# S5 input weights from two turned factors that are read back from DRAM with replication, in a hybrid encoder layer on Trainium2

## The chip, the cores and the metric

The kernel runs on one core of one Trainium2 chip. The metric is the device time of one execution in microseconds (us); the median of the runs is compared. The engines are TensorE (PE, whose weight loads are the row PEld), VectorE (DVE), ScalarE (ACT), GpSimd (POOL) and SyncE (SP). SP and POOL issue the DMAs.

## The reference, cut to what matters

One encoder layer over 512 tokens of 1024 channels: an input projection, two mixers in parallel (a bidirectional S5 state-space branch and a gMLP branch), a gated merge, cross-attention to 256 memory tokens, a SwiGLU FFN and a final norm, all in float32. The change is in the S5 branch. Its 512 channels are 32 groups (G) of 16 channels (C); each group has 64 complex states for each of two directions, so the 128 partitions hold direction and state.

```python
def s5_scan(u, lam_re, lam_im, log_step, b_re, b_im, c_re, c_im, reverse):
    lam = lax.complex(lam_re, lam_im)
    step = jnp.exp(log_step)[:, None]
    lam_bar = jnp.exp(lam * step)
    b_bar = ((lam_bar - 1.0) / lam)[..., None] * lax.complex(b_re, b_im)
    bu = jnp.einsum('gpc,lbgc->lbgp', b_bar, u)
    _, states = lax.associative_scan(_linear_recurrence, (a, bu), axis=0, reverse=reverse)
    return jnp.einsum('gcp,lbgp->lbgc', lax.complex(c_re, c_im), states).real
...
y = jax.nn.gelu(y); y = y * jax.nn.sigmoid(y @ w_glu)
merged = gate_a * (ya @ w_proj_a) + gate_b * (yb @ w_proj_b)
```

## The kernel before, in words

**The dense products.** Each float32 product is three products of split operands: ACT casts a weight block to fp32r (`whi`, L85), DVE makes the rest (`wlo`, L86), and PE takes hi x hi, hi x lo and lo x hi. Weight blocks of 512 KB stand in one `plan`. `next_w` hands out the next block; on the way it begins loads three blocks ahead (`LOADS`) and splits two blocks ahead (`SPLITS`). Three raw buffers rotate, so a load on SP's queue waits until the split of three blocks before has read its buffer.

**The weight sums.** w_proj_b, w_q and w_down use seven products in place of eight and need sums of weight blocks. `plan_sums` gives each of its 40 jobs a place in the plan and a step: at the place SP copies one block from DRAM to DRAM (L288), and `step` places later POOL adds another one by an accumulating DMA (L289). The first sixteen jobs are for w_proj_b and w_q. The plan's places run: 0 to 3 half of the v projection, 4 to 7 `u`, 8 to 11 the other half of v, 12 to 19 gate a, 20 to 27 the gMLP's u, 28 to 35 gate b, 36 to 49 w_proj_b, 50 and 51 w_glu.

**The S5 work beside them.** `s5_program` is a generator. `tick(us)` is called after each block with the PE time of that block; it grants credits at a rate of 0.8, and each `yield` of the generator spends some. A `yield None` gives up the rest of a tick. `later(n, f)` runs `f` after n units of 5.2 us of such product time. Thus the order in which instructions are written is fixed; a scheduler then places each engine's instructions by readiness in its own timeline, with that order as the priority. `in_order` pins an instruction, and `behind(ins, first)` orders one instruction after another on the same queue without a semaphore.

**The S5 inputs.** The scan is over 64 chunks of 8 steps (`Q`). For each chunk the state input is a product of u (128 rows: channel and step in the chunk) with weights W[(c, l), (direction, state)] for each group, real and imaginary. The weights are b_bar[state, c] times lam_bar's power [state, l]. Groups are taken in four octaves of eight (`NO`, `GO`). Before, `s5_inputs` makes for each octave and each of the two parts the weights with the state on the partitions: two broadcast products and a sum on DVE over 128 x 1024 (`inner` spreads b over l, `outer` the powers over c; L972, L974, L976), in the tile `wsx`. Then `turn` transposes the eight 128 x 128 blocks on PE (L951) and ACT copies them out of PSUM into `wt` (L952); `apply` multiplies with u (L958, tile `pz`); `keep` puts the result into `zh`, half by ACT (L963) and half by DVE (L964). An octave waits until the octave before has been turned.

**What follows.** When all eight halves are in `zh`, `s5_scan` runs 62 steps of four small DVE operations (L985 to L988). `s5_outputs` makes the outputs of each octave (`py` L1014, transposes `pyt` L1029, `y` L1034). `store_outputs` takes the gelu (L1046) and stores y to DRAM by POOL (`yd`, L1049). It is called three times between w_proj_b's products and once after `finish_side`, which runs out what is left. Then the tile `ygt` is loaded from `yd` by POOL (L1343), split (`yg_hi` L1349, `yg_lo` L1350), and w_glu's products read it.

`s5_kernels` makes the weights inside a chunk: `e` tiles (tags e0 and e1, two buffers each), the products `pk`, and for octaves 2 and 3 copies of e to DRAM (`ed`, L875) that are read back later. Slot A of SBUF holds `xt` at first, then `squares` (layer norm), then `sv`; slot E holds `wsx`.

Of the kernel before, what the change touches and what calls it, by code (L numbers as in the profile page):

```python
# [9 lines left out]
F32 = mybir.dt.float32  # L10
F32R = mybir.dt.float32r
AF = mybir.ActivationFunctionType
ALU = mybir.AluOpType
# [4 lines left out]
P = 128  # L18
D = 1024
T = 512  # L20
NT = T // P
# [18 lines left out]
Q = 8  # L40
# [12 lines left out]
def hybrid_layer_kernel(  # L53
# [26 lines left out]
    def aux(name, shape=(P, 512)):  # L80
        return pa.tile(list(shape), F32, tag="aux", name=name)
# [30 lines left out]
        cast[0] = split(hi, lo, src)  # L112
        return hi, lo

    cast = [None]

    def behind(ins, first):

# [20 lines left out]
    def plan_block(w, kb, k, c0, n, place=None, ordered=False, then=None, parts=1):  # L139
        got = {}  # L140

        def load():
            got["raw"] = wp.tile([P, k, n], F32, tag="raw", name="wraw", bufs=3)
            for i in range(0, k, k // parts):
                ins = nc.sync.dma_start(got["raw"][:, i:i + k // parts], block(w, kb + i, k // parts, c0, n))
                if ordered:
                    in_order(ins)

        def make():
# [182 lines left out]
    for i in range(4):  # L332
# [5 lines left out]
    plan_down(w_down, lambda q, c: down_tokens[0](q, c), down_plan)  # L338
    plan_units(UNITS, down_plan)

    plan_sums([(5, 3), (7, 3), (9, 2), (13, 5), (14, 5), (16, 4)] + [(18 + 2 * i, 3) for i in range(8)] +
              [(51 + 2 * i, 2) for i in range(4)] + [(85 + 3 * i, 3) for i in range(3)] +
              [(95 + 2 * i, 2) for i in range(3)] + [(122 + 4 * i, 4) for i in range(16)])
    used_w = [0]
# [112 lines left out]
    def later(n, fn):  # L457

        side["later"].append((side["now"] + n, fn))
# [228 lines left out]
    def s5_setup():  # L688
# [88 lines left out]
        st["pe"], st["pw"] = [], []  # L777
        for src in (pr, pi):
            pe = s5p.tile([P, G, Q], F32, name="pe%d" % len(st["pe"]))
            pw = s5p.tile([P, G, Q], F32, name="pw%d" % len(st["pw"]))  # L780
            A_.copy(pe[lo_], src[lo_, :, 0:Q])
            V.tensor_copy(pe[hi_], src[hi_, :, 0:Q][:, :, ::-1])
            V.tensor_copy(pw[lo_], src[lo_, :, 1:Q + 1])
            A_.copy(pw[hi_], src[hi_, :, 1:Q + 1][:, :, ::-1])
            st["pe"].append(pe)
            st["pw"].append(pw)
        ca = s5p.tile([P, 2, G], F32, name="ca")
        cb = s5p.tile([P, 2, G], F32, name="cb")
        for i in range(2):
# [35 lines left out]
        for t in st["bd"]:  # L825
            nc.gpsimd.memset(t, 0.0)
# [20 lines left out]
    def lc(t, g):  # L847
        return t[:, g].rearrange("p a b -> p (a b)")
# [84 lines left out]
            nc.sync.dma_start(glc(e), ed[o][i])  # L933
        load(o, es)

    turned = set()

    def s5_inputs(o):

        gs = slice(o * GO, (o + 1) * GO)  # L940
        br, bi = st["b"]
        pr, pi = st["pw"]
        zh, u = st["zh"], st["u"]

        def turn(i, e):
            turned.add((o, i))
            wt = s5p.tile([P, GO, P], F32, tag="wt", name="wt", bufs=2)
            for hf in range(2):
                ps = aux("pw", (P, 4, P))
                for j in range(4):  # L950
                    nc.tensor.transpose(ps[:, j, :], lc(e, 4 * hf + j), ident)  # L951
                nc.scalar.copy(wt[:, 4 * hf:4 * hf + 4, :], ps)  # L952
            later(0.5, lambda: apply(i, wt))

        def apply(i, wt):
            ps = aux("pz", (P, GO, NCH))
            for g in range(GO):
                nc.tensor.matmul(ps[:, g, :], wt[:, g, :], u[:, o * GO + g, :], start=True, stop=True)  # L958
            zv = zh[:, :, i, gs].rearrange("p n g -> p g n")
            later(0.5, lambda: keep(zv, ps))  # L960

        def keep(zv, ps):
            nc.scalar.copy(zv[lo_], ps[lo_])  # L963
            V.tensor_copy(zv[hi_], ps[hi_, :, ::-1])  # L964
            st["nz"] = st.get("nz", 0) + 1

        for i in range(2):
            while o > 0 and (o - 1, i) not in turned:
                yield None
            e = wsx[:, 2 + i].rearrange("p g (c l) -> p g c l", c=C)  # L970
            w = s5p.tile([P, GO, C, Q], F32, tag="etmp", name="etmp2")
            V.tensor_tensor(e, inner(br, gs, Q), outer((pr, pi)[i], gs, C), ALU.mult)  # L972
            yield 1.1
            V.tensor_tensor(w, inner(bi, gs, Q), outer((pi, pr)[i], gs, C), ALU.mult)  # L974
            yield 1.1
            V.tensor_tensor(e, e, w, (ALU.subtract, ALU.add)[i])  # L976
# [148 lines left out]
    tokm(w_in, OFF_V + 512, xn, KD, zv_evac(1))  # L1125


    squares = slot("A", (P, NT, GW), F32, "squares")

    def layer_norm(t):  # L1130

        nm, ss, ms, r = (np_.tile([P, 1 + (k == "ss")], F32, tag=k, name=k, bufs=2) for k in ("nm", "ss", "ms", "r"))
        nc.vector.tensor_tensor(nm, zsum[:, t, 0:1], zsum[:, t, 1:2], ALU.add)
        nc.vector.tensor_scalar(nm, nm, -1.0 / GW, None, ALU.mult)
        z = zt[:, t, :]
        for i in range(2):
            sum_sq(ss[:, i:i + 1], z[:, HALF[i]], squares[:, t, HALF[i]], nm)
# [861 lines left out]
```

## Time and profile before

| what | value |
|---|---|
| median of 3 runs | 866.23 us (866.2 to 868.49) |
| the profiled execution | 865.49 us, its span 863.7 us |
| granted TensorE clock | 0.998 |
| PE, DVE, ACT, POOL busy | 99%, 76%, 54%, 10% of the span |
| DMA | 169.56 MB in 115752 packets |
| HBM | 159.71 MB read, 48.73 MB written |

The times are those of whole executions; all views come from the one profiled execution, whose span runs from the first to the last instruction. Busy PE time is modelled: a product's tail overlaps with the next product, so the starts, not the durations, tell what one costs. In the lines of groups, the number after the bar is the group's busy time in us, then the mean of one in ns, then the idle time of the engine just before it and what ended most of that.

### The profile page before, as it was taken

To read this page: it belongs to the slowest core of one execution; us is meant where nothing else is said; L and a number is where in the kernel's file an instruction comes from. 1 tells how busy PE (TensorE), PEld (TensorE's weight loads), DVE (VectorE), ACT (ScalarE), POOL (GpSimd) and SP (SyncE) were. 2 spreads that over 40 slices of the span, in tenths; PEclk is the share of its full clock that TensorE was granted. 3 is DMA by queue.
4 is the path that set the end of the run, shared out by engine and by line. 5 is a ranking of instruction groups with operands and counts; after the bars stand their busy time and mean duration, and the time that the engine had idled before them with its cause. 6 is when DMAs were issued, how large, how long until landed. Compare 5 with 4: busy or idle time off the path is not lost.

```text
span 863.7 us, 14764 instructions
## 1 busy us (share of the span) xinstructions
PE 856.1 (99%) x5780; PEld 766.6 (89%) x5780; DVE 660.5 (76%) x1076; ACT 466.1 (54%) x698; POOL 89.3 (10%) x119
## 2 busy tenths in 40 slices
PE   9999999999999999999999999999999999999997
PEld 7888888888889988889899888999999999988886
DVE  7698896899846768668758755867877768899875
ACT  6734853244355543557547544645545554656674
POOL 0002302111021110110010001010211111000000
PEclk9999999999999999999999999999999999999999
DMA  9759565987574798735696555557999898366564
GB/s 270 196 174 308 113 174 153 254 195 191 146 220 150 244 309 248 244 102 199 213 276 162 147 146 147 146 159 185 213 233 240 215 229 220 92 191 209 196 186 156
DMA packets 115752, 169.56 MB, mean 196 GB/s; under 512 B 9297, under 2 KB 80481, under 8 KB 115554
## 3 DMA queue, kind: packets, MB, share of 16 engines
q1 hardware_dynamic: 95330, 139.54, 49.3%
q0 software_dynamic: 20064, 28.55, 20.4%
q8 instruction: 45, 0.74, 0.3%
q10 hardware_dynamic: 288, 0.52, 0.2%
q14 instruction: 25, 0.20, 0.1%
HBM read 159.71 MB, written 48.73 MB: 241 GB/s over the span
## 4 chain that ended last, share of the span: by engine, by line
PE 99%; DVE 1%; ACT 0%; issue 0%
PE pf L374 27%; PE pt L374 18%; PE px L1238 13%; PE dx L374 7%; PE pq L1238 6%; PE dq L374 3%; PE pv L1238 3%; PE bx L1238 3%; PE qx L1238 3%; PE dv L374 2%; PE pz L958 2%; PE qv L1238 1%; PE po L374 1%; PE psc L374 1%; PE py L1014 1%; PE qq L1238 1%
## 5 line engine op out<-in xcount | busy, mean ns | idle before, releaser
L85 ACT CAST whi<-wraw 128x1024 fp32r<-128x1024 f32 x141 | 145.2, 1031 | 160.2 <-PE pf L374 54.8
L86 DVE TENSOR_TENSOR wlo<-wraw,whi 128x1024 fp32r<-128x1024 f32 x141 | 168.3, 1195 | 64.8 <-ACT whi L85 64.2
L374 PE MATMUL pf<-xn,whi 128*128 128x512 f32 x448 | 140.1, 392 | 0.0
L374 PEld LDWEIGHTS pf<-xn,whi 128*128 128x128 f32 x448 | 83.5, 188 | 16.9
L374 PE MATMUL pf<-xn,wlo 128*128 128x512 f32 x224 | 87.5, 391 | 0.0
L1238 PE MATMUL px<-fn,whi 128*128 128x256 f32 x480 | 83.4, 277 | 0.0
L1238 PEld LDWEIGHTS px<-fn,whi 128*128 128x128 f32 x480 | 72.5, 188 | 0.2
L86 DVE TENSOR_TENSOR wlo<-b,whi 128x1024 fp32r<-128x1024 f32 x40 | 48.9, 1223 | 26.0 <-ACT whi L85 26.0
L85 ACT CAST whi<-b 128x1024 fp32r<-128x1024 f32 x40 | 42.2, 1054 | 48.3 <-PE px L1238 27.7
L1238 PE MATMUL px<-fn,wlo 128*128 128x256 f32 x240 | 66.4, 277 | 0.0
L1238 PE MATMUL pq<-s,whi 128*128 128x256 f32 x320 | 55.0, 276 | 0.0
L374 PE MATMUL dx<-whi,s 128*128 128x512 f32 x166 | 52.2, 391 | 0.4 <-DVE h L1922 0.4
L86 DVE TENSOR_TENSOR wlo<-t,whi 128x1024 fp32r<-128x1024 f32 x30 | 36.7, 1225 | 18.4 <-ACT whi L85 18.4
L85 ACT CAST whi<-t 128x1024 fp32r<-128x1024 f32 x30 | 31.6, 1054 | 34.6 <-PE pv L1238 11.4
L374 PEld LDWEIGHTS pf<-xn,wlo 128*128 128x128 f32 x224 | 42.1, 188 | 8.7
L1238 PEld LDWEIGHTS pq<-s,whi 128*128 128x128 f32 x320 | 48.2, 188 | 0.0
L1238 PEld LDWEIGHTS px<-fn,wlo 128*128 128x128 f32 x240 | 45.1, 188 | 0.0
L1238 PE MATMUL pq<-s,wlo 128*128 128x256 f32 x160 | 44.2, 276 | 0.0
L374 PE MATMUL pt<-whi,xn 128*128 128x512 f32 x128 | 43.1, 402 | 0.0
L374 PEld LDWEIGHTS dx<-whi,s 128*128 128x128 f32 x166 | 31.1, 188 | 7.4 <-ACT whi L85 0.8
L374 PE MATMUL dx<-wlo,s 128*128 128x512 f32 x83 | 32.2, 389 | 0.0
L289 POOL DMA_DIRECT2D dsum<-in_w_down_dram x12 | 13.2, 1103 | 172.5 <-DMA dsum<-in_w_down_dram 167.4
(458 smaller groups left out, 2222.7 us busy)
## 6 DMA issues: line engine op xcount, KB each, us to landing
wraw<-in_w_in_dram SPq DMA_DIRECT2D x34, 512.0 KB, 4.6
dsum<-in_w_down_dram SPq DMA_DIRECT2D x20, 512.0 KB, 5.8
wraw<-dsum SPq DMA_DIRECT2D x20, 512.0 KB, 4.4
b<-in_w_gate_dram SPq DMA_DIRECT2D x15, 512.0 KB, 5.1
b<-in_w_up_dram SPq DMA_DIRECT2D x15, 512.0 KB, 4.7
wraw<-in_w_down_dram SPq DMA_DIRECT2D x15, 512.0 KB, 3.8
dsum<-in_w_down_dram POOLq DMA_DIRECT2D x10, 512.0 KB, 7.5
dsum<-dsum POOLq DMA_DIRECT2D x10, 512.0 KB, 7.9
```

Of the source, the lines that this page charges most:

```text
L85: hi = nc.scalar.copy(dst_hi, src)
L86: lo = nc.vector.tensor_tensor(dst_lo, src, dst_hi.bitcast(F32), ALU.subtract)
L289: plan[j + step][1].append((0, lambda d=dst, x=more: nc.gpsimd.dma_start(d, x, accum_op=ALU.add)))
L374: m = nc.tensor.matmul(ps, a[x], b[y], start=start and i == 0, stop=stop and i == 2, skip_group_check=free)
L958: nc.tensor.matmul(ps[:, g, :], wt[:, g, :], u[:, o * GO + g, :], start=True, stop=True)
L1014: in_order(nc.tensor.matmul(ps[64 * j:64 * j + 64, :, :, h, :].rearrange("p q d c -> p d q c"), a, b, start=k == ks[0], stop=k == ks[2], t ...
L1238: nc.tensor.matmul(ps[:, j, :], a[x], b[y], start=start and j == k == i == 0, stop=k == 3 and i == 2, skip_group_check=True)
```

## The change

The weights W are a product of two factors that depend on (c, state) and on (l, state). After the change each factor is turned once and written to DRAM with the state in the free direction; for each octave it is loaded back with replication, so that both lie in the layout (c, l) x (group, state), and DVE's two products and the sum give the weights already turned.

- In `s5_setup` the powers `pw` are laid out by octave, step and group, turned by four transposes and stored (`ptd`). `by_octave` copies b's real and imaginary part into that order, turns each by four transposes, and stores it (`btd`). The set-up yields 1.9 credits more.
- `load_factors(o)` issues four loads of 512 KB on SP for an octave: b with each row repeated over the eight steps, the powers with their eight rows repeated over the 16 channels. Even octaves go into slot A (`scr`) and `wsx`, odd ones into the e buffers. Octave 0 is loaded after the set-up, octave 1 one unit after u is there, octaves 2 and 3 three units after the inputs of 0 and 1 are written. The later ones are ordered behind the weight load that was issued last.
- `s5_inputs` has no `turn` any more: `apply` reads the sum itself.
- `plan_sums`: twelve of the first fourteen places move to later ones.
- Slot A is `scr` from the start of the S5 work on; the layer norm's squares of all four token tiles go to its first part.

```diff
-    plan_sums([(5, 3), (7, 3), (9, 2), (13, 5), (14, 5), (16, 4)] + [(18 + 2 * i, 3) for i in range(8)] +
+    plan_sums([(5, 3), (7, 3)] + [(15 + 2 * i, 3) for i in range(10)] + [(40, 3), (44, 3)] +
               [(51 + 2 * i, 2) for i in range(4)] + [(85 + 3 * i, 3) for i in range(3)] +
...
-            pw = s5p.tile([P, G, Q], F32, name="pw%d" % len(st["pw"]))
+            pw = s5p.tile([P, NO, Q, GO], F32, name="pw%d" % len(st["pw"]))
             A_.copy(pe[lo_], src[lo_, :, 0:Q])
             V.tensor_copy(pe[hi_], src[hi_, :, 0:Q][:, :, ::-1])
-            V.tensor_copy(pw[lo_], src[lo_, :, 1:Q + 1])
-            A_.copy(pw[hi_], src[hi_, :, 1:Q + 1][:, :, ::-1])
+            rows = pw.rearrange("p o q g -> p o g q")
+            by_octave = src[:, :, 1:Q + 1].rearrange("p (o g) q -> p o g q", o=NO)
+            V.tensor_copy(rows[lo_], by_octave[lo_])
+            A_.copy(rows[hi_], by_octave[hi_, :, :, ::-1])
...
+        yield 0.1
+        ps = aux("pbt", (P, 2, 2, P))
+        for i in range(2):
+            for k in range(2):
+                nc.tensor.transpose(ps[:, i, k, :], st["pw"][i].rearrange("p o q g -> p (o q g)")[:, P * k:P * k + P], ident)
+        rows = scr[:, 3, 0:512].rearrange("p (i k d) -> p i k d", i=2, k=2)
+        A_.copy(rows, ps)
+        for i in range(2):
+            nc.sync.dma_start(ptd[i].rearrange("(k q) d -> q k d", k=2), rows[:, i])
...
+        def by_octave(i, z):
+            t = scr[:, 1 + i, 0:512].rearrange("p (o c g) -> p o c g", o=NO, c=C)
+            A_.copy(t.rearrange("p o c g -> p o g c"), z.rearrange("p (o g) c -> p o g c", o=NO))
+            ps = aux("pbt", (P, NO, P))
+            for o in range(NO):
+                nc.tensor.transpose(ps[:, o, :], t[:, o].rearrange("p c g -> p (c g)"), ident)
+            rows = scr[:, 1 + i, 512:1024].rearrange("p (o d) -> p o d", o=NO)
+            A_.copy(rows, ps)
+            nc.sync.dma_start(btd[i].rearrange("o q d -> q o d"), rows)
...
         yield 1.8
+        by_octave(0, zr)
...
+        yield 1.8
+        by_octave(1, zi)
...
+    btd = [dp.tile([NO, P, P], F32, name=f"btd{i}") for i in range(2)]
+    ptd = [dp.tile([NO * Q * GO, P], F32, name=f"ptd{i}") for i in range(2)]
+    factors = {}
+
+    def load_factors(o):
+
+        if o % 2 == 0:
+            fs = [scr[:, 1], scr[:, 2], wsx[:, 2].rearrange("p h d -> p (h d)"), wsx[:, 3].rearrange("p h d -> p (h d)")]
+        else:
+            fs = [s5p.tile([P, GO * P], F32, tag=f"e{i % 2}", name="fac", bufs=2) for i in range(4)]
+        first = last_load[0]
+        for i in range(2):
+            for x, dst, steps in ((btd[i][o], fs[i], [(GO * P, C), (0, Q)]),
+                                  (ptd[i][o * Q * GO:(o + 1) * Q * GO], fs[2 + i], [(0, C), (GO * P, Q)])):
+                ins = nc.sync.dma_start(dst, type(x)(x.tensor, x.offset, steps + [(1, GO * P)],
+                                                     dep_tracking_offset=x.dep_tracking_offset))
+                if o:
+                    behind(ins, first)
+        factors[o] = fs
...
-        def turn(i, e):
-            turned.add((o, i))
-            wt = s5p.tile([P, GO, P], F32, tag="wt", name="wt", bufs=2)
-            for hf in range(2):
-                ps = aux("pw", (P, 4, P))
-                for j in range(4):
-                    nc.tensor.transpose(ps[:, j, :], lc(e, 4 * hf + j), ident)
-                nc.scalar.copy(wt[:, 4 * hf:4 * hf + 4, :], ps)
-            later(0.5, lambda: apply(i, wt))
...
-            while o > 0 and (o - 1, i) not in turned:
-                yield None
-            e = wsx[:, 2 + i].rearrange("p g (c l) -> p g c l", c=C)
-            w = s5p.tile([P, GO, C, Q], F32, tag="etmp", name="etmp2")
-            V.tensor_tensor(e, inner(br, gs, Q), outer((pr, pi)[i], gs, C), ALU.mult)
+            e = s5p.tile([P, GO * P], F32, tag="wt", name="wt", bufs=2)
+            w = s5p.tile([P, GO * P], F32, tag="etmp", name="etmp2")
+            V.tensor_tensor(e, br, (pr, pi)[i], ALU.mult)
             yield 1.1
-            V.tensor_tensor(w, inner(bi, gs, Q), outer((pi, pr)[i], gs, C), ALU.mult)
+            V.tensor_tensor(w, bi, (pi, pr)[i], ALU.mult)
             yield 1.1
             V.tensor_tensor(e, e, w, (ALU.subtract, ALU.add)[i])
             yield 1.1
-            later(1, lambda i=i, e=e: turn(i, e))
+            later(1, lambda i=i, e=e: apply(i, e))
+        if o + 2 < NO:
+            later(3, lambda: load_factors(o + 2))
...
         yield from s5_setup()
+        load_factors(0)
         for o in (2, 3):
             yield from s5_kernels(o)
...
+        later(1, lambda: load_factors(1))
         for o in range(NO):
+            while o not in factors:
+                yield None
             yield from s5_inputs(o)
...
+    scr = slot("A", (P, 4, 1024), F32, "scr")
...
-    squares = slot("A", (P, NT, GW), F32, "squares")
```

More of the change, by code (lines that the diff above doesn't have):

```diff
@@ L113, in halves @@
         return hi, lo
-    cast = [None]
+    cast, last_load = [None], [None]
     def behind(ins, first):
@@ L147, in load @@
                     in_order(ins)
+                last_load[0] = ins
         def make():
@@ L934, in reload @@
         load(o, es)
-    turned = set()
+    btd = [dp.tile([NO, P, P], F32, name=f"btd{i}") for i in range(2)]
[15 more added lines that the diff above has]
+        factors[o] = fs
     def s5_inputs(o):
         gs = slice(o * GO, (o + 1) * GO)
-        br, bi = st["b"]
-        pr, pi = st["pw"]
+        br, bi, pr, pi = factors.pop(o)
         zh, u = st["zh"], st["u"]
-        def turn(i, e):
-            turned.add((o, i))
-            wt = s5p.tile([P, GO, P], F32, tag="wt", name="wt", bufs=2)
-            for hf in range(2):
-                ps = aux("pw", (P, 4, P))
-                for j in range(4):
-                    nc.tensor.transpose(ps[:, j, :], lc(e, 4 * hf + j), ident)
-                nc.scalar.copy(wt[:, 4 * hf:4 * hf + 4, :], ps)
-            later(0.5, lambda: apply(i, wt))
         def apply(i, wt):
@@ L957, in apply @@
             for g in range(GO):
-                nc.tensor.matmul(ps[:, g, :], wt[:, g, :], u[:, o * GO + g, :], start=True, stop=True)
+                nc.tensor.matmul(ps[:, g, :], wt[:, g * P:(g + 1) * P], u[:, o * GO + g, :], start=True, stop=True)
             zv = zh[:, :, i, gs].rearrange("p n g -> p g n")
@@ L1136, in layer_norm @@
         for i in range(2):
-            sum_sq(ss[:, i:i + 1], z[:, HALF[i]], squares[:, t, HALF[i]], nm)
+            sum_sq(ss[:, i:i + 1], z[:, HALF[i]], scr[:, 0, HALF[i]], nm)
         nc.vector.tensor_tensor(ms, ss[:, 0:1], ss[:, 1:2], ALU.add)
```

## The prediction, made before the change had run

> **What bounds the kernel now.** I read the page first, then who TensorE (PE) waited for, then the busy time by stretches around the S5 inputs, then the tiles and the order of time. The page's head:
>
> ```profile
> span 863.7 us, 14764 instructions
> PE 856.1 (99%) x5780; PEld 766.6 (89%) x5780; DVE 660.5 (76%) x1076; ACT 466.1 (54%) x698; POOL 89.3 (10%) x119
> ```
>
> PE's waits (line, what it waited for, total us, times, longest), all of them:
>
> ```profile
> PE pt L573 <- DVE ones L493: 1.1, 1, 1.1
> PE dx L374 <- DVE h L1922: 0.4, 1, 0.4
> PE ptr L635 <- issue: 0.2, 1, 0.2
> PE ptr L635 <- DVE ms L618: 0.2, 1, 0.2
> ```
>
> So PE waits 1.9 us in the whole run, none of it between 36 and 840 us: any PE time removed there is time removed from the end, unless something else then arrives late. The stretches in which the S5 inputs are made (PE, PEld, DVE, ACT, POOL busy us; clock; DMA share; GB/s):
>
> ```profile
> 60.00:84.00 24.00, 24.00 (x237) 19.38 (x236) 21.05 (x23) 9.99 (x21) 6.24 (x10) 1.00 1.06 313
> ...
> 108.00:132.00 24.00, 24.00 (x148) 21.04 (x147) 22.14 (x19) 12.87 (x20) 2.58 (x4) 1.00 0.62 178
> ```
>
> PE is full in each, VectorE (DVE) nearly so, and the DMA engines are full in the first.
>
> **Part 1, the transposes removed.** The operations on pw (min/median/max ns, first and last start), and PE in order of time around two groups of eight transposes:
>
> ```profile
> L951 PE MATMUL pw<-ident,wsx x64: 270/273/328, 75.4 to 127.1; 128*128 128x128 f32 x64
> L952 ACT COPY wt<-pw x16: 563/587/652, 76.8 to 128.0; 128x512 f32<-128x512 f32 x16
> ...
> 75.36 1.09 PE L951 MATMUL pw<-ident,wsx 128*128 128x128 f32 x8
> 76.21 0.70 PE L374 MATMUL pt<-whi,xn 128*128 128x512 f32 x2
> 76.75 0.40 PE L374 MATMUL pt<-wlo,xn 128*128 128x512 f32 x1
> 76.99 0.62 PE L374 MATMUL pt<-whi,xn 128*128 128x512 f32 x2
> 77.45 0.39 PE L374 MATMUL pt<-wlo,xn 128*128 128x512 f32 x1
> ...
> 82.83 1.04 PE L951 MATMUL pw<-ident,wsx 128*128 128x128 f32 x8
> 83.63 0.71 PE L374 MATMUL pt<-whi,xn 128*128 128x512 f32 x2
> ```
>
> A transpose lasts 273 ns, but they overlap: eight start at 75.36 and the next product starts at 76.21, 0.85 us later; the second group takes 83.63 - 82.83 = 0.80 us. I take 0.825 us a group. The pair of products right behind a group takes 76.75 - 76.21 = 0.54 us where the next pair takes 77.45 - 76.99 = 0.46 us, so each group costs 0.08 us more. 64 transposes in eight groups: 8 x (0.825 + 0.08) = 7.24 us. Added are 2 x 4 (the b factors, by `by_octave`) and 4 (the powers), 12 in three groups: 12 x 0.103 + 3 x 0.08 = 1.48 us. Net on PE: -5.75 us. Bounds: without the switching cost 52 x 0.103 = -5.4 us; by busy time, which also counts each group's tail that lies under the next product, 52 x 8.7/64 = -7.1 us:
>
> ```profile
> L951 PE MATMUL pw<-ident,wsx 128*128 128x128 f32 x64 | 8.7, 274 | 0.0
> ```
>
> I keep the value from the starts, since only a start moves the next product. The Trainium skill (TensorE: Matmul & The Clock Gate, Part 4: PE-mode transpose) gives about 275 ns for a 128x128 transpose in bf16 inside a kernel; the trace's 273 ns for fp32 agrees as a duration, and taken as a price it would make the change worth an estimated 52 x 0.275 = 14.3 us.
>
> **Part 2, VectorE and ScalarE.** The 24 products and sums of the inputs stay 24, now contiguous on both sides instead of broadcast. The rows of a broadcast product and of the contiguous sum:
>
> ```profile
> L972 DVE TENSOR_TENSOR wsx<-bbr,pw x8: 1214/1220/1227, 49.8 to 115.5; 128x1024 f32<-128x1024 f32 x8
> ...
> L976 DVE TENSOR_TENSOR wsx<-wsx,etmp 128x1024 f32<-128x1024 f32 x8 | 9.8, 1221 | 0.1
> ```
>
> 1220 and 1221 ns: no gain and no loss. The four copies of the powers change layout only. ScalarE (ACT) loses 16 x 0.587 = 9.4 us (L952) and gains two strided copies and three evictions of 512 columns, each between L952's 0.587 us and the 1.114 us of the strided eviction
>
> ```profile
> L734 ACT COPY raw_c<-pbc 128x512 f32<-128x512 f32 x2 | 2.2, 1114 | 0.0
> ```
>
> so 5 x 0.587 = 2.9 to 5 x 1.114 = 5.6 us. Neither engine is on the path: zero, below zero excluded because no PE wait here ends on ACT.
>
> **Part 3, the DMAs.** Added on SP's queue: four stores of 768 KB in all, and 16 loads of 512 KB, four for each octave, 8.4 MB. Rows of like transfers (KB each, median us to landing):
>
> ```profile
> wraw<-in_w_in_dram SPq DMA_DIRECT2D x34, 512.0 KB, 4.6
> ed<-e SPq DMA_DIRECT2D x4, 512.0 KB, 6.3
> e<-ed SPq DMA_DIRECT2D x4, 512.0 KB, 8.2
> ```
>
> One load lands in 4.6 to 8.2 us, four in a row in not less than 2.1 MB / 313 GB/s = 6.7 us; I take 9. Octave 0's loads are issued right after the set-up; what hides them is the wait for `u`, which octave 0 needs anyway, and if that is gone they cost one octave's price of the second rival. Octave 1's need the e buffers, which are free when the copies `ed<-e` have landed; octaves 2 and 3 reuse the buffers of 0 and 1 and are issued (`later(3)`) three ticks before they are wanted, behind a weight load. They delay VectorE, not PE, as long as the products pz are put late enough on PE. What SP's queue holds behind a factor load that waits is the next weight load, and its landing is early: the block loaded at 77.57 is cast first at 90.58.
>
> ```profile
> 77.57 1.60 SPq L145 DMA_DIRECT2D wraw<-in_w_in_dram  x2
> ...
> 90.58 1.04 ACT L85 CAST whi<-wraw 128x1024 fp32r<-128x1024 f32 x1
> ...
> SPq L875 <- DVE etmp L974: 5.9, 1, 5.9
> ```
>
> That is 13 us of cover for the weights, where the one wait of this kind in before, the copy `ed<-e` held on SP by VectorE (last row), was 5.9 us. The weight sums leave the stretch 60 to 84 us, whose DMA share is 1.06, and two of them move to places 40 and 44, among w_proj_b's blocks. I cost the loads at 0, bounds 0 to 12 us (second rival).
>
> **Part 4, the hand-over to the GLU.** This is where the cover is thin. By the yields the set-up now costs 1.9 more credits, and followed tick by tick through the generator the scan and the outputs come one tick later; octave 3's y is stored only after `finish_side`, two products of 2.72 us (5.4 us of PE work, first row below) later than before. PE is 5.75 us early by then, so the store falls at about the same absolute time and PE comes to it 5.75 us sooner. The rows of before, from the chain (the product) and the order of time:
>
> ```profile
> 280.12 2.72 PE qv L1238 x24
> 281.92 1.20 POOL L1049 DMA_DIRECT2D yd<-y  x2 [1.47 <-ACT y L1046]
> ...
> 296.10 0.68 DVE L1350 TENSOR_TENSOR yg_lo<-ygt,yg_hi 128x512 fp32r<-128x512 f32 x1
> 297.67 0.62 ACT L1349 CAST yg_hi<-ygt 128x512 fp32r<-128x512 f32 x1 [0.71 <-DMA ygt<-yd]
> 298.20 2.06 ACT L85 CAST whi<-wraw 128x1024 fp32r<-128x1024 f32 x2
> 299.71 1.22 DVE L86 TENSOR_TENSOR wlo<-wraw,whi 128x1024 fp32r<-128x1024 f32 x1
> 301.72 0.39 PE L374 MATMUL pf<-yg_hi,whi 128*128 128x512 f32 x1
> ```
>
> PE would want the GLU's first product at 301.72 - 5.75 = 295.97. The first yg_lo ends at 296.10 + 0.68 = 296.78: a stall of 0.8 us at the least. If the cast of the GLU's weights stays behind the last yg_hi, their low half ends at 299.71 + 1.22 = 300.93 and is used two products (0.46 us) after the start: 300.93 - 0.46 - 295.97 = 4.5 us at the most. The weights' cast waits for nothing of S5 and can go first, so I take 1 us.
>
> **The sum.** The profiled execution took 865.49 us, 1.8 us of it outside the span. 865.49 - 5.75 + 1.0 = 860.74. It lies 0.74 us under the median of 866.23, so 861.5 us is forecast for the median.
>
> **The rivals.**
>
> First: the hand-over takes back nearly all. For it: S5's outputs are bound to program order, the reload of y is serial (store, landing, load, cast), and a weight sum at place 43 now puts an accumulating DMA in POOL's queue just then. In this trace small stores by POOL that follow such a DMA land in 7.7 to 8.0 us, and in 3.6 to 3.9 without one near (stores at 70.8 and at 152.3):
>
> ```profile
> 69.47 1.17 POOL L289 DMA_DIRECT2D bsum<-in_w_proj_b_dram  x1 [30.96 <-DMA bsum<-in_w_proj_b_dram]
> L911 POOL DMA_DIRECT2D kd<-ks x4: 484/494/521, 70.8 to 72.3; - x4
> DMA to landing us min/median/max: 7.7/7.9/8.0
> ...
> L911 POOL DMA_DIRECT2D kd<-ks x4: 502/504/504, 152.3 to 153.7; - x4
> DMA to landing us min/median/max: 3.6/3.9/3.9
> ```
>
> The Trainium skill (DMA: Bandwidth & Descriptors, SWDGE vs HWDGE vs iDMA) says that GpSimd's DMAs have a single queue, so the stores would stand behind the sum; the trace agrees with that by the pair above. Against it: place 43 can be through before. Price: stall 4.5 us, 865.49 - 5.75 + 4.5 + 0.74 = 865.0; with 4 us for the sum in front, 869.0.
>
> Second, on the slower side: the factor loads are late where PE stands in order. The pz products follow the third VectorE operation of their half at once now; if the order on PE was laid out for landings of 5 us and four loads take 9, PE stands about 4 us at the first pz of octaves 1, 2 and 3: +12 us, 865.49 - 5.75 + 1 + 12 + 0.74 = 873.5. It makes the kernel slower by 0.3% from 2.5 us an octave on. For it: the full DMA share in 60 to 84 us, and buffers that chain each octave's load to an earlier octave's last read. Against it: the sums that leave, and a PE order that puts pz a tick behind its operands.
>
> Third: PE does better than packed, nothing is late: 860.5, inside the forecast's own range of 859.1 (866.23 less the busy-time bound) to 863.5 (3 us at the hand-over).
>
> Fourth: transposes are worth their whole duration, 273 ns by L951's row: 865.49 - 52 x 0.273 + 0.74 = 852.0. The starts 0.103 us apart speak against it.
>
> **How the numbers follow.** 0.3% of 866 us is 2.6 us, about what a measurement of this kernel can tell from no change; faster means under 863.6, slower over 868.8. Forecast with its third variant 0.60; first rival 0.20 (most of it within 0.3%); second 0.17; fourth 0.03. Faster 0.60 + 0.03 = 0.63, same 0.20, slower 0.17. The range takes the forecast from its low bound and the first rival up to its end with a sum in front: 859 to 869, leaving out the second and fourth, 0.20.
>
> **What would show it.** Right: 12 transposes of the new kind and none at the inputs; PE's busy time 5 to 6 us less; TT rows of the inputs still at 1.22 us; at most one new PE wait, of about 1 us, at the first GLU product, ended by yg_lo or the weights' cast. First rival: that wait is 4 us or more. Second: PE waits at pz ended by VectorE, and VectorE's by loads of the factors. I am wrong altogether if PE's waits stay at 1.9 us and the span still shrinks by less than 5 us.

## The result: slower by 1.3%, and the profile after

The changed kernel takes 878.84 us (median of 4 runs, 875.96 to 880.27); the kernel before took 867.36 us beside it. The ratio is 1.0128, 95% interval 1.0111 to 1.0145. 861.5 us was forecast, with a range of 859 to 869. The profiled run took 879.03 us, 877.1 of it span.

The page's head after the change, with the granted clock by slices:

```profile
span 877.1 us, 14685 instructions
...
PE 860.3 (98%) x5728; PEld 767.8 (88%) x5728; DVE 661.7 (75%) x1076; ACT 461.8 (53%) x687; POOL 86.9 (10%) x119
...
PEclk9999969999999999999999999999999999999999
```

52 instructions fewer on TensorE, yet 4.2 us more busy: one slice of PEclk has a 6 where every slice stood at 9 before. PE's waits (line, what it waited for, total us, times, longest):

```profile
PE pz L991 <- DVE wt L1007: 4.9, 1, 4.9
PE py L1047 <- DVE ss L1035: 2.5, 1, 2.5
PE ptr L535 <- ACT full L541: 1.2, 1, 1.2
...
PE pf L375 <- ACT yg_hi L1385: 0.4, 1, 0.4
```

None of these four is in the profile before. The first, in PE's order of time, and what VectorE was doing then:

```profile
106.62 0.62 PE L375 MATMUL pf<-xn,whi 128*128 128x512 f32 x2
...
109.11 0.39 PE L375 MATMUL pf<-xn,wlo 128*128 128x512 f32 x1
114.36 3.65 PE L991 MATMUL pz<-u,wt 128*128 128x64 f32 x16 [4.86 <-DVE wt L1007]
...
122.60 1.05 PE L375 MATMUL pf<-xn,whi 128*128 128x512 f32 x2
```
```profile
110.72 1.23 DVE L1005 TENSOR_TENSOR etmp<-fac 128x1024 f32<-128x1024 f32 x1 [3.38 <-DMA fac<-ptd]
...
112.99 1.22 DVE L1007 TENSOR_TENSOR wt<-wt,etmp 128x1024 f32<-128x1024 f32 x1
```

PE comes to the first pz of octave 1 at 109.5 and stands 4.86 us for VectorE's third operation, whose factor (fac, octave 1) has just landed. Behind the stand, pz takes 3.65 us for 16 products, and a pair of products 1.05 us where it took 0.62 before. The stretches, coarse and fine (busy us of PE, PEld, DVE, ACT, POOL; clock; DMA share; GB/s):

```profile
84.00:108.00 24.00, 24.00 (x124) 20.47 (x123) 8.87 (x19) 16.68 (x28) 1.65 (x3) 1.00 1.02 254
108.00:132.00 24.00, 19.14 (x86) 16.82 (x85) 20.19 (x18) 7.31 (x8) 1.79 (x2) 0.72 1.06 301
...
109.50:112.00 2.50, 0.00 (x0) 0.00 (x0) 1.28 (x2) 0.00 (x0) 0.00 (x0) 1.00 1.04 221
...
114.40:125.65 11.25, 11.25 (x43) 10.29 (x44) 11.16 (x10) 4.51 (x5) 0.00 (x0) 0.50 1.06 278
125.65:132.00 6.35, 6.35 (x38) 5.54 (x37) 5.39 (x6) 2.57 (x3) 1.79 (x2) 1.00 1.08 379
```

The stretch ahead of 108 in the profile before:

```profile
84.00:108.00 24.00, 24.00 (x141) 20.93 (x140) 21.62 (x37) 21.11 (x39) 6.68 (x5) 1.00 0.59 130
```

VectorE now does 8.87 us of work there, where it did 21.62: it is waiting. The DMA share stays over 1.0 up to 132, where it was 0.59 and then 0.62. And PE's clock is halved from 114.4 to 125.65 (by the trace's record from 112.03, for 13.65 us): 11.3 us of PE work at half speed is 5.7 us lost. VectorE is as full there: its sum for the second pz ends at 117.74, and PE comes to it at 118.33, so at the full clock PE would have come sooner and stood again. The 5.7 us are what the ledger books, not what a full clock alone would have given back.

The ledger. At the last psv product, behind all S5 inputs, the kernel is 6.0 us late (168.99 against 163.01), 0.8 of that from the start of the run. The rest, 5.2 us, is -5.3 (52 transposes; summed from start to next start, 64 took 6.50 us before, 12 take 1.23 now) + 4.86 (stand) + 5.7 (clock) = 5.3. From there to the end of the program 7.6 us more: 4.5 up to the end of w_proj_b's products (2.5 of it the stand at py; the other 2.0 stay open), 0.9 up to the end of the GLU's, 1.2 at ptr, the rest in small gaps.

Why the factor was late shows in SP's order of time and in the landings (KB each, median us), after:

```profile
54.81 1.24 SPq L976 DMA_DIRECT2D wsx<-ptd  x2
56.17 1.82 SPq L976 DMA_DIRECT2D scr<-btd  x2
...
58.04 0.59 SPq L289 DMA_DIRECT2D bsum<-in_w_proj_b_dram  x1
...
64.30 2.14 SPq L289 DMA_DIRECT2D bsum<-in_w_proj_b_dram  x1
66.53 1.72 SPq L1156 DMA_DIRECT2D ud<-xa  x1
...
70.53 0.55 SPq L976 DMA_DIRECT2D fac<-btd  x1
...
73.11 6.98 SPq L936 DMA_DIRECT2D kd<-ks  x4
...
81.47 0.55 SPq L976 DMA_DIRECT2D fac<-btd  x1
...
84.80 0.76 SPq L1160 DMA_DIRECT2D u<-ud  x1
85.66 8.77 SPq L936 DMA_DIRECT2D kd<-ks  x2
94.53 0.55 SPq L976 DMA_DIRECT2D fac<-ptd  x1
...
98.61 0.54 SPq L976 DMA_DIRECT2D fac<-ptd  x1
```
```profile
ed<-e SPq DMA_DIRECT2D x4, 512.0 KB, 11.8
fac<-btd SPq DMA_DIRECT2D x4, 512.0 KB, 8.2
fac<-ptd SPq DMA_DIRECT2D x4, 512.0 KB, 12.1
ud<-xa SPq DMA_DIRECT2D x4, 256.0 KB, 13.4
```

In before the four stores of u landed in a median of 2.9 us and the load of `u` was issued at 66.07; now they take 13.4, and the load goes out at 84.80. The copy `ed<-e` takes 11.8 us instead of 6.3, and the e buffers, which octave 1's factors need, come free that much later. SP's queue also stood: one of the two small stores at 85.66 (16 KB, `kd`) took 8.31 us to issue, where no `kd` store of SP took over 1.35 us before, and octave 1's last two loads were issued behind it. No run takes that apart.

### The profile page after: what moved, and what is told of

It is laid out like the page before. It is cut to its first block, busy times and chain, and to the rows that moved or that the text cites. A ratio compares the mean times of both kernels' runs of the same rounds, so it can differ in the third digit from the quotient of the medians.

```text
span 877.1 us, 14685 instructions
## 1 busy us (share of the span) xinstructions
PE 860.3 (98%) x5728; PEld 767.8 (88%) x5728; DVE 661.7 (75%) x1076; ACT 461.8 (53%) x687; POOL 86.9 (10%) x119
## 4 chain that ended last, share of the span: by engine, by line
PE 90%; DMA 3%; DVE 3%; ACT 2%; issue 1%; SPq 1%; POOL 0%; POOLq 0%; ACTq 0%
PE pf L375 24%; PE pt L375 15%; PE px L1274 12%; PE dx L375 6%; PE pq L1274 6%; PE pv L1274 3%; PE dq L375 3%; PE qx L1274 2%; PE dv L375 2%; PE bx L1274 2%; PE pz L991 2%; DMA fac<-ptd 1%; PE qv L1274 1%; PE py L1047 1%; PE po L375 1%; PE psc L375 1%
## 5 line engine op out<-in xcount | busy, mean ns | idle before, releaser
L501 ACT ACTIVATE sq<-h 128x512 f32<-128x512 f32 x23 | 14.5, 630 | 31.2 <-DVE h L1464 25.7
```

What stands on the lines that cost most here:

```text
L501: act = nc.scalar.activation(sq[:, :src.shape[-1]], src, AF.Square, bias=bias, accum_out=dst)
```

## The experiments

All ratios are to the kernel before, timed beside the run (its medians lay between 866.86 and 867.76 us).

**Fewer loads.** First, octaves 1 to 3 multiply octave 0's factors: 12 of the 16 loads are left out.

```diff
     def load_factors(o):
+        if o:
+            factors[o] = st["fs"]
+            return
...
-        factors[o] = fs
+        factors[o] = st["fs"] = fs
```

> The changed kernel, in which octaves 1 to 3 use octave 0's factors again: 12 of the 16 factor loads (6.3 MB) are left out, so its values are not the reference's; everything else stays. Theory A (the loads crowd the DMA engines between 57 and 130 us; landings of 10 to 13 us make S5 late, PE stands 4.9 us at a pz and then runs some 13 us at half clock): the wait at pz is under 1 us, the granted clock stays 1.0, the first pz starts before 90 us instead of 96, and the time is 862 to 869 us. Theory B (S5 is late because its set-up costs one tick more and PE's order was laid out wrongly, the loads matter little): PE still waits 3 us or more at a pz, and the time is 874 us or more.

868.69 us, ratio 1.0020 (1.0004 to 1.0036), as theory A had it, though the stand at pz is 1.6 us and the first pz starts at 93.77. The clock stays at 1.0 in the profiled run and 10 us have come back; what is left is still not faster than before. Next, the loads of the powers alone are left out for octaves 1 to 3 (10 loads), and then all of them:

```diff
+                if o and dst is fs[2 + i]:
+                    continue
                 ins = nc.sync.dma_start(dst, ...)
```
```diff
+        fs = [scr[:, 1], scr[:, 2], scr[:, 2], scr[:, 1]]
-        for i in range(2):
+        for i in range(0):
```

> The kernel after with the powers' loads of octaves 1 to 3 left out (octave 0's powers are multiplied, the output is not the reference's): 10 loads, where after has 16 and the first run of this kind 4. If every load costs the same: 868.7 + (878.8 - 868.7) x 6 / 12 = 873.7. If only a stand of several us at pz, with the clock that it halves, makes the loss: two loads land in about half the time of four, no stand over 2 us, 869 to 871.

> The kernel after without any factor load (every octave multiplies the staging rows that lie in SBUF already, the output is not the reference's); the stores and the 12 transposes stay. Theory A: with nothing in the way of u the PE waits at pz are gone, and 52 transposes fewer are all that is left, less about 1.3 us for the sums at places 40 and 44: 862 to 865. Rival C (the set-up's stores and turned layouts, or the order of the rest of the program, eat the gain): 866.5 or more, with waits that don't end on a load.

With ten loads 874.04 us (1.0082, 1.0066 to 1.0098), the even share for every load; without any 863.12 us (0.9953, 0.9934 to 0.9972). The waits without loads, all over 0.2 us:

```profile
PE bx L1273 <- ACT u L1291: 1.6, 1, 1.6
PE pt L574 <- DVE ones L494: 1.1, 1, 1.1
PE dx L375 <- DVE h L1957: 0.4, 1, 0.4
```

With 0, 4, 10 and 16 loads: 863.1, 868.7, 874.0, 878.8 us, 0.8 to 1.4 us a load. Without any, the gain that was forecast is there: at the last psv product this kernel is 4.7 us ahead of before although its run began 1.1 us later, so 5.8 us came off TensorE. So the set-up's stores and layouts cost nothing that shows. The powers' loads are left out together with their e buffers, so these three runs change bytes, waits and the chain of buffers at once.

**Loads that nobody reads.** Is it the bytes, or the wait for them? The 12 loads of the first run issued all the same, into DRAM, octave 0's factors still multiplied; then octave 0's four alone, with nothing read; and 16 such transfers put into the kernel before, at the same points.

```diff
-            fs = [s5p.tile([P, GO * P], F32, tag=f"e{i % 2}", name="fac", bufs=2) for i in range(4)]
+            fs = [ldst[o - 1, i] for i in range(4)]
...
-        factors[o] = fs
+        factors[o] = st.setdefault("fs", fs)
```

> The kernel after, all octaves multiplying octave 0's factors (the output is not the reference's), but the other 12 loads still issued at the same points, into DRAM, read by nothing. It stands between the run with 4 loads (868.7 us) and after (878.8 us). Theory A (crowding): 874 to 879, waits at pz or py stay. Rival D (the wait for the data): 868 to 870, as with 4 loads.

> The run without any factor load (863.1 us; the output is not the reference's), with octave 0's four loads issued after all, into DRAM, read by nothing. Theory A1 (u is late behind these loads): 866.5 to 868.7, with a PE wait at pz or py. Rival A2 (it is the wait for their data that makes octave 0 late): 863 to 864.5, about 0.25 us a load, as the 12 unread loads cost 1.1 us.

```diff
+    def extra_loads(o):
+        for i in range(4):
+            ins = nc.sync.dma_start(ldst[o, i], w_in[P * i:P * i + P, GO * P * o:GO * P * (o + 1)])
```

> The kernel before, unchanged in its arithmetic, with 16 transfers of 512 KB (DRAM to DRAM, read by nothing) put on SP's queue where the changed kernel issues its factor loads. Theory A (the bytes crowd every other transfer of S5, u, ks and xa among them): slower by 3 us or more, with u issued later than 66 us and a PE wait at pz or py. Rival D (only the wait for the factors themselves costs): within 1 us of before, no new PE wait over 0.5 us.

With 12 unread 869.82 us (1.0030, 1.0019 to 1.0042), as the rival had it; with octave 0's four unread 865.94 us (0.9988, 0.9980 to 0.9997), between the two expectations; and with 16 transfers in the kernel before 868.45 us (1.0014, 1.0004 to 1.0024), near the rival. The transfers were as slow as in after and held up the copies of e nearly as much, the stores of u somewhat less (7.2 and 9.6 us, after 13.4); here the rows with 12 unread, then with octave 0's four:

```profile
ldst<-btd SPq DMA_DIRECT2D x6, 512.0 KB, 13.1
ldst<-ptd SPq DMA_DIRECT2D x6, 512.0 KB, 12.4
ed<-e SPq DMA_DIRECT2D x4, 512.0 KB, 11.4
```
```profile
ed<-e SPq DMA_DIRECT2D x4, 512.0 KB, 11.1
ud<-xa SPq DMA_DIRECT2D x4, 256.0 KB, 9.6
```

Yet 12 of them cost 869.82 - 868.69 = 1.1 us when nothing waits for them (the intervals of the two runs overlap), and 878.84 - 869.82 = 9.0 us more when VectorE does. So for octaves 1 to 3 it is the wait that costs and not the bytes, as the rival held. Two things come with the wait and are not separated from it: an unread load waits for no buffer, and PE's order is laid out anew in every kernel. In the records 327 products with xn stand ahead of the first pz after the change, 341 with 12 unread loads, 306 with four loads, 268 without any and 266 before.

Octave 0's four cost 2.8 us unread (865.94 - 863.12), 2.8 us more when read. They stand ahead of `u`, which was issued at 80.39 with them and at 70.08 without. How much of the first 2.8 us is due to that place is not shown: at the last psv product the kernel with them is 1.3 us later, and 1.2 us are a wait at ptr, 370 us behind it.

**The weight sums.** The sums at their old places in after, the new places alone in before, and later places in after:

```diff
-    plan_sums([(5, 3), (7, 3)] + [(15 + 2 * i, 3) for i in range(10)] + [(40, 3), (44, 3)] +
+    plan_sums([(17 + 2 * i, 3) for i in range(10)] + [(37, 3), (39, 3), (41, 3), (44, 3)] +
```

> The changed kernel with the places of the weight sums of before (5, 7, 9, 13, 14, 16, 18 and so on). Theory A: two to three more sums lie in the crowded stretch, landings get longer, PE's waits between 60 and 160 us grow from 4.9 to 8 us or more, and the time is 882 to 890 us. Theory B: within 2 us of the changed kernel's 879.

> The kernel before with the new places of the weight sums and nothing else of the change. Both theories: PE is gap-free there either way, 864 to 869 us, no difference that counts; were the new places 40 and 44 harmful by themselves, a PE wait of 1 us or more would show at the GLU's first product (302 us) and the time would be 868 us or more.

> The changed kernel with the first sums moved out of the crowded stretch too: places 17, 19, 21 and so on in place of 5, 7, 15, 17. Theory A: the landings between 57 and 95 us fall from 10 to 13 us to under 9, the load of u is issued before 78 us instead of 84.8, the wait at pz falls under 2 us, the clock stays at 1.0 and the time is 862 to 870 us. Theory B: within 2 us of the changed kernel's 879.

In this order 881.38 us (1.0171, 1.0155 to 1.0186), 868.51 us (1.0019, 1.0009 to 1.0028), 870.81 us (1.0052, 1.0032 to 1.0072). The move of the sums is worth 2.5 us to the changed kernel and costs the old one 0.2%; the first run lies between its two expectations, and its longest stand is 5.4 us at py, not at pz. Clearing the two early sums out as well (with places 15 and 40) is worth 8 us, nearly as much as leaving out 12 loads: `u` goes out at 75.79. That is just over what theory A expected, because one stand is left, at octave 3, and the clock again drops behind it (columns as above):

```profile
120.60:124.20 3.60, 0.73 (x7) 0.76 (x7) 3.54 (x4) 1.68 (x3) 0.93 (x1) 1.00 0.24 38
124.20:131.00 6.80, 6.80 (x23) 5.80 (x22) 6.74 (x7) 1.06 (x1) 0.54 (x3) 0.50 0.96 216
```

Without loads the old places give 864.97 us, 1.9 us over the new ones:

> The run without any factor load (863.1 us; the output is not the reference's), with the weight sums at their old places. If the new places cost about 1.3 us here too, as in the old kernel: 861.5 to 862.3. Rival: the old places crowd u's stretch, 863.5 to 865.

This fits the rival, that the new places crowd u's stretch less.

**Cures that failed.** On top of the later sums: octave 3's pz one tick later, then the factor loads a tick earlier, then four sums moved past the GLU; and the last two with octave 0's factors for all.

```diff
-            later(1, lambda i=i, e=e: apply(i, e))
+            later(2 if o == 3 else 1, lambda i=i, e=e: apply(i, e))
...
-            later(3, lambda: load_factors(o + 2))
+            later(2, lambda: load_factors(o + 2))
...
-              [(51 + 2 * i, 2) for i in range(4)] +
+              [(51 + 2 * i, 2) for i in range(8)] +
```

> The kernel after with the sums at places 17 to 35, 37, 39, 41 and 44 (870.8 us as measured), and the pz products of octave 3 put one tick later into TensorE's order. Theory A (PE stands in order behind factor loads, and the clock halves after it): the PE wait of 2.9 us at pz ended by VectorE goes, the clock stays at 1.0 around 124 us, where the 6.8 us at half clock cost about 3.4 us; together about 6 us, so 864.5 to 866. Rival B (the S5 chain is late as a whole, the stand at pz is only where it shows first): the time comes back at py or at the GLU's first product, whose wait grows from 1.5 us to 4 us or more; 869 to 871.

> The kernel of the run before in this list, with the factor loads of octaves 2 and 3 issued two ticks after the inputs before them and not three; counted through the generator the scan and the outputs then come one tick (5.2 us of TensorE work) earlier, back to where they were before the change. Theory A: the wait at the GLU's first product (1.5 us ended by yg_hi) falls under 0.5 us; 1 to 1.5 us below the run before. Rival: the loads now wait on SP's queue for VectorE's last read of their buffers and hold the next weights; a new PE wait of 1 us or more ended by the weights' cast or low half between 100 and 140 us; same or slower.

> The kernel of the run before in this list, with the four sums of places 37 to 44 moved to places 51 to 65. Theory A': sums around the GLU cost about 1.3 us (the old kernel with the new sums was slower by 0.19%), so about 1 to 1.5 us below the run before. Rival: the sums are as dear behind the GLU as in front of it, or late for w_q: same within 0.5 us, or a new wait at w_out or w_q.

> All octaves multiply octave 0's factors, so 12 of the 16 factor loads are left out (the output is not the reference's), and the sums stand as in the run before in this list, the load tick too. Theory A: with no factor load in the way, what is left of the change is 52 transposes fewer on TensorE; the waits of the first such run (2.6 at pz, 1.1 at yg_hi, 1.2 at ptr) shrink to about 2 together; 861.5 to 864. Rival C: the stores and turned layouts of the set-up, or the later u, cost the rest by themselves: 866 or more, with the pz wait at u still there.

In this order 872.89 (1.0056, 1.0035 to 1.0077), 877.82 (1.0114, 1.0087 to 1.0142), 872.07 (1.0055, 1.0034 to 1.0076) and 868.35 us (1.0002, 0.9986 to 1.0018). All four expectations of theory A missed, and the rivals' places were mostly wrong too. Moving one pz on PE only moves the stand: 2.3 us at another pz, with the clock at 0.50 behind it for 6.4 us. The scan a tick earlier brings PE to py before its operands:

```profile
PE py L1047 <- DMA tt<-kd: 3.4, 1, 3.4
PE pz L991 <- DVE ms L1175: 2.6, 1, 2.6
```
```profile
252.36 1.15 POOL L290 DMA_DIRECT2D qsum<-in_w_q_dram  x1 [10.43 <-DMA qsum<-in_w_q_dram]
...
253.76 2.80 POOL L952 DMA_DIRECT2D tt<-kd  x4
...
264.36 0.53 POOL L952 DMA_DIRECT2D tt<-kd  x1 [5.98 <-DMA qsum<-in_w_q_dram]
```

The loads of tt stand in POOL's queue behind a weight sum, which itself stood 10.43 us for the transfer that it adds to. The Trainium skill (DMA: Bandwidth & Descriptors, SWDGE vs HWDGE vs iDMA) gives GpSimd's DMAs one queue; the trace agrees: the sum landed 11.7 us after its issue, at 264.06, the seven loads of tt behind it landed only after that (10.4 to 11.1 us each), and the one issued at 264.36 took 5.2. With the four sums of this stretch moved past the GLU the stand at py is gone, and 5.75 us come back (872.07). In the last of the four the stand at pz is 1.8 us, ended by wt, and its runs spread over 7 us (864.50 to 871.54), so it adds nothing to the first run of its kind.

**Loads in time.** Octaves 0 and 1 made by transposes as before, octaves 2 and 3 by factors in buffers that are free since the set-up; octave 2's are asked for right behind `u`, octave 3's when octave 1's first half has been turned. 32 transposes go, 6 come, 8 loads stay.

```diff
+        fs = [scr[:, 1], scr[:, 2], scr[:, 3]] if o == 2 else []
+        while len(fs) < 4:
+            fs.append(s5p.tile([P, GO * P], F32, tag=f"e{len(fs) % 2}", name="fac", bufs=2))
+        if o == 3:
+            fs[3] = wsx[:, 2].rearrange("p h d -> p (h d)")
...
-                if o:
-                    behind(ins, first)
+                behind(ins, st["ui"] if o == 2 else first)
```

> Whole computation: octaves 0 and 1 by transposes as before, octaves 2 and 3 by loaded factors in buffers free since the set-up (three rows of scr, four of the e buffers, one of wsx), asked for right behind u and some 15 us ahead of use; sums at the old places. 32 transposes go and 6 come: TensorE saves 4 x 0.905 - 6 x 0.103 - 3 x 0.08 = 2.8 us. Theory A (lateness): no wait at pz over 1 us, eight loads of which none is waited for cost 8 x 0.09 = 0.7 us, so 2 us below before. Rival: any load of 512 KB costs 0.9 us wherever it is put (as 4, 10 and 16 loads read off): 8 x 0.9 - 2.8 = 4.4 us above before.

> The hybrid with the sums at places 17 to 35, 37, 39, 41 and 44. If u's stretch profits more from the empty queue than the GLU's stretch loses: below the hybrid with the old places, by up to 1 us; if the late places cost 1.3 us as in the old kernel: 1 to 1.5 us above it.

872.09 us (1.0059, 1.0047 to 1.0071) and 870.14 us (1.0039, 1.0025 to 1.0053). The first is near the rival's 4.4 us above before, but a row gives another reason: octaves 0 and 1 read the powers in the new layout with a stride of 32 bytes, and each of their eight products took some 2.1 us.

```profile
L1017 DVE TENSOR_TENSOR wsx<-bbr,pw x4: 2103/2120/2144, 51.4 to 92.2; 128x1024 f32<-128x1024 f32 x4
```

The Trainium skill (SBUF — State Buffer, Door 1: The DMA port swizzle, its note on 16-byte lines) says that fp32 strided past four elements pays; this row, 2.12 us for the 1.22 us of the contiguous layout, agrees. With the powers of octaves 0 and 1 back in their old layout:

```diff
+            old = pw[:, 0:P].rearrange("p (g q) -> p g q", q=Q)
+            V.tensor_copy(old[lo_], src[lo_, 0:2 * GO, 1:Q + 1])
+            A_.copy(old[hi_], src[hi_, 0:2 * GO, 1:Q + 1][:, :, ::-1])
```

> The hybrid with the sums as in after, and the powers of octaves 0 and 1 kept in their old layout, so that all products take 1.22 us again (in the first hybrids eight of them took 2.04 to 2.10 us). Theory A (only late loads cost): the run without loads gave 863.1 us with 5.75 us off TensorE; here 2.8 us come off it and eight loads lie in the queue, 0.1 us each: 863.1 + 2.95 + 0.8 = 866.9, the same as before within 1 us, no wait at pz over 1 us. Rival (any load costs 0.9 us): 863.1 + 2.95 + 7.2 = 873.3.

> The same with the sums at places 17 to 35, 37, 39, 41 and 44. In after these places were worth 8.1 us, because they emptied u's stretch; if that stretch is no longer the bound here, the difference from the run before in this list is under 1.5 us.

866.65 us (0.9988, 0.9974 to 1.0001) and 866.27 us (0.9992, 0.9976 to 1.0008). The second differs from the 870.14 us above in the layout alone, which was thus worth 3.9 us. For the first 866.9 was expected from the terms (863.1 with nothing to load, 2.95 for the transposes kept, 0.8 for eight loads of which none is late); the rival that every load costs 0.9 us gave 873.3 and falls. That the sum came within 0.3 us is in part luck: the runs spread from 864.05 to 869.95, and in the profiled one, the slowest, no pz waits for a factor, but two stand 0.88 and 0.78 us for a transposed block, 3.41 us at half clock follow, and ptr waits 1.2 us, none of which is a term. With u's stretch no longer the bound, the places of the sums are worth 0.4 us here, not 8. The products are back at their old price:

```profile
L1021 DVE TENSOR_TENSOR wsx<-bbr,pw x4: 1208/1217/1226, 51.1 to 85.9; 128x1024 f32<-128x1024 f32 x4
```

These are the best whole versions tried. By the prices of the transposes they save 2.8 us of PE (an estimate), and neither can be told from the kernel before.

## Why the prediction was wrong, by its own steps

**Part 1 held.** -5.75 us was forecast. The starts give -5.3, and the run without loads 5.8 at the last psv product. The fourth rival (273 ns each, 852.0 us) falls: with no load in the way 863.1 us is reached.

**Part 2 held.** The contiguous products take as long as the broadcast ones, the evictions 0.59 to 0.60 us:

```profile
L1003 DVE TENSOR_TENSOR wt<-fac x4: 1217/1218/1220, 103.6 to 137.3; 128x1024 f32<-128x1024 f32 x4
...
L836 ACT COPY scr<-pbt x2: 592/600/607, 52.6 to 53.0; 128x512 f32<-128x512 f32 x2
L796 ACT COPY scr<-pbt x1: 588/588/588, 52.1 to 52.1; 128x512 f32<-128x512 f32 x1
```

The two strided copies took 1.20 us each, a little over their bound; the five together 4.2 us, inside it. No wait of PE ends on them.

**Part 3 is the step that failed,** in three terms and a premise. "I take 9" for four loads: octave 1's four were issued one by one between 70.53 and 98.61, as the e buffers came free and SP's queue let them, and the last landed at 110.69. With the early sums out of the way four of them, issued in a row from 100.54 on, still landed only at 117.39, 16.9 us. A bandwidth worked out for 2.1 MB alone was no price in a stretch whose DMA share was already 1.06. "What hides them is the wait for `u`", of octave 0's loads: they stand ahead of u's last stores in the same queue and themselves made `u` late, by 10.3 us at its issue; unread they cost 2.8 us, of which 1.3 are there behind the S5 inputs. And "I cost the loads at 0" rested on pz lying late enough on PE, which no row showed: it was a guess on the side of the change. The cover of 13 us that was named did hold: no wait of PE in this stretch ends on a dense weight block. It covered the wrong consumer. And that the weight sums leave the stretch 60 to 84 us came true only in part: places 5 and 7 stayed, with copies on SP at 58.04 and 64.30 and additions on POOL at 68.13 and 80.07, and clearing them out (with two other places) brought 8 us.

**The second rival came nearest.** Its place and its signs are what the profile shows: PE waits at pz ended by VectorE, VectorE's by the factors. Its price was 12 us over the forecast (873.5), 17.3 us were measured. It counted three stands of 4 us; there was one, of 4.86. It left out that the clock halves behind it (5.7 us), that S5's lateness shows a second time at py (2.5), and the small losses behind. It got a chance of 0.17, and the range stopped short of it. What spoke for it, a full DMA share and a chain of buffers, was read from rows; what spoke against it was not: an order on PE that was not looked at, and sums that leave, two of which stayed. On these rows it deserved more than 0.17.

**Part 4 and the first rival.** The stand at the GLU was forecast at 1 us, and 0.4 is there; S5's lateness had been paid before, at pz and py. The queue on POOL that the first rival feared does bite, at tt and not at y's store, in the run whose scan comes a tick earlier. The pair of rows by which the prediction showed it was misread, though: the stores at 152.3, taken as having no such DMA near, stand 3.1 us behind one.

```profile
149.16 1.20 POOL L289 DMA_DIRECT2D qsum<-in_w_q_dram  x1 [0.53 <-issue]
```

It landed after 6.3 us, at 155.5, and the stores landed right behind it, as those at 70.8 did behind theirs (issued at 69.47, landed after 9.0 us, at 78.5). So both groups fit one queue; the group without a sum near is the one at 146.7, with 3.3 to 3.9 us.

**What stays open.** The ptr wait of 1.2 us (0.2 to 1.2 in most variants, the kernel before with extra transfers among them) comes with another order of ScalarE's and PE's work some 400 us later; no run took it apart. Nor was the half clock separated from the stand that it goes with, or the wait for the factors from the buffers they wait for and from the order on PE that each kernel has of its own. Why one store's issue on SP took 8.31 us is open too.

## What to carry to other kernels

A transfer's price in a crowded stretch is its landing there, behind what its queue and the engines already hold, not its bytes over the bandwidth: look first at the DMA share of the stretch where it is issued, and at who is next in its queue. The same 12 loads cost 1.1 us when nothing waited for them and 10.1 us when VectorE did, with PE in order behind it. Where an in-order engine is full, a late operand of a small step stops the large one beside it, so work saved on that engine counts only when the replacement is there in time; and a saving of 52 short transposes is worth their starts, 5.3 to 5.8 us here, which is less than one such stand with the half clock behind it (4.86 + 5.7 us).

## What the runs showed of the hardware that was not expected

**The clock falls with short stands.** Stands of 1.69 (the first hybrid), 1.87, 2.26, 2.90 and 4.86 us went with 6.83, 3.41, 6.83, 6.83 and 13.65 us at half clock, by the trace's record, all multiples of 3.41; they begin between 2.3 us ahead of the stand's end and 2.1 us behind it. One of 2.19 us in the run with 12 unread loads, the one of 2.53 us at py after the change and one of 3.40 us at py in the run whose scan comes a tick earlier went with none, while in the third hybrid two stands of 0.88 and 0.78 us, 1.1 us apart, went with 3.41 us. So the length of a stand alone does not decide; what does is not shown. The stretches behind the stands of 1.87 us (ten loads) and 2.19 us:

```profile
129.00:132.40 3.40, 3.40 (x10) 2.63 (x9) 3.34 (x4) 0.95 (x1) 0.00 (x0) 0.50 1.01 311
```
```profile
95.80:103.00 7.20, 7.20 (x39) 6.20 (x40) 2.11 (x9) 6.29 (x11) 1.10 (x2) 1.00 1.08 324
```

The Trainium skill (TensorE: Matmul & The Clock Gate, Part 1) gives a free-running window of 3413 ns; the lengths agree with it. Its working rule there, no idle gap of more than about 3.4 us (HAM oscillation), is too mild for this kernel: a gap of 1.69 us was enough.

**Unread transfers are nearly free.** 8.4 MB more of them in the kernel before cost 1.2 us (0.14%), though its first pz came 6.5 us later (87.64 against 81.10).
